# Attention for 64 heads on one core: pair 1 transposed head by head, score blocks dealt out anew, group 120 shared by two engines, a written order in place of a planner

## The chip, the cores and the metric

The kernel runs on one core of a Trainium2 chip. A core has five engines that run side by side, each with its own list of instructions: TensorE (PE in the profile, with its weight loads as PEld), VectorE (DVE), ScalarE (ACT), GpSimd (POOL) and SyncE (SP, which here only issues DMAs). The metric is the device time of one execution in microseconds; lower is better.

## The reference

For 64 heads (8 batches of 8) of 512 rows and 64 columns, in float32:

```python
scale = 1.0 / np.sqrt(q.shape[-1])
scores = np.einsum('bhqd,bhkd->bhqk', q, k) * scale
scores = scores - scores.max(axis=-1, keepdims=True)
attn = np.exp(scores)
attn = attn / attn.sum(axis=-1, keepdims=True)
return np.einsum('bhqk,bhkd->bhqd', attn, v).astype(np.float32)
```

## The kernel before

**Tiling.** Heads go in 32 pairs, a (h = 0) and b (h = 1). A pair's q and k are loaded as 256 KB each, cast to f16 by GpSimd (`cast`, L525), transposed by TensorE through an identity (`transposes`, L558) into PSUM, and copied by VectorE to `tqk` (`copy`, L571): 64 partitions for head a, 64 for head b. A score block is 128 keys by 512 queries of one head, one matmul with 64 contracted rows (`scores`, L598). Two blocks make a group of 128 x 1024 scores in one of three PSUM buffers `st`. In most pairs a group holds chunk c of head a and of head b, whose two matmuls lie in different row halves of the array; in pairs 0 and 31 it holds two chunks of one head. The 128 groups, 0 to 127, are taken in order; the last is done in two halves of 256 queries (numbers 127 and 128).

**Two ways to the exponential.** For 112 groups ScalarE reads `st` and writes `pt`, f16 (L602; L801 for the first three). For the 16 groups in `ON_DVE` VectorE does it from the bits of the number: `raise_` (L625) reads `st` and writes `pd`, then come five passes in SBUF (`pass_`, L642 to L665), which leave two factors, `pe` and `pd`, that TensorE uses as two blocks.

**Values.** A unit is 128 queries of one head: four matmuls of 65 columns (L704), one for each key chunk, and one more for each chunk that VectorE did. The 65th column sums the weights. Seven units fill a PSUM bank; VectorE takes a reciprocal (L671) and multiplies into a ring in SBUF (L676), from which SyncE stores. Values wait in the list until TensorE has time: `pt` has 24 buffers. The last head (31b) has its own matmuls (`last_values`, L720), reciprocal, product and store (L733, L734, L740); the two stores before it go out by ScalarE's queue.

**Order.** `Plan.run` steps through a model of the engines with fixed costs and writes the list of steps down; `do[what](*args)` (L867) issues them under a manual schedule, so that each engine works through its own part of that list in order. `KNOWN` names exponentials that also wait for an old GpSimd cast; a cast may be told to wait for a VectorE instruction (`cast_behind`, L539).

**Start.** Pair 0 is loaded by halves, and `first_pair` does its q and k through short steps of its own. Pair 1's q and k are loaded whole; k is cast by GpSimd, q half by VectorE (L523) and half by GpSimd (L524); k and q of both heads are transposed and copied one after the other (L565), and the first scores of pair 1 (group 4) need all of it.

Of the kernel before, what the change touches and what calls it, by code (L numbers as in the profile page):

```python
# [17 lines left out]
class Plan:  # L18

    SLOT, EXP, EXP_DONE, EXP_FIXED = 216, 853, 181, 64  # L20
    INTO, OUT_OF = 96, 96
    TRANSPOSE, V_UNIT = 222, 128
    TO_ACT, TO_DVE, TO_PE = 220, 210, 60

    COPY, NORM, RAISE = (601, 690), (50, 133), (1132, 1215)
    RECIPROCAL = 115
    SCALE, PRODUCT, EXTRA = 333, 600, 29
    COPY_1 = (400, 190)
    NORM_COLUMN, PASS_DONE = 67, 115
    PASSES = (SCALE, SCALE, PRODUCT, SCALE, PRODUCT)  # L30
    BITS = 2
    NEEDS = (None, None, 0, 2, 3)
    FIRST_EXP = 5000
    STEP = 5
    CALM, KEEN = 9000, 4
    FIRST_UNIT = 4
    KNOWN, OVER = (13, 15, 18, 20, 22, 24, 27, 42, 50, 61, 69, 97), 6
    ON_DVE = (5, 10, 16, 25, 28, 39, 44, 54, 63, 66, 74, 81, 91, 96, 103, 116)

    LATE_NORM, LATE_COPY, HURRY, SOON, BACKLOG = 700, 1500, 800, 160, 600  # L40
    LATE_MUL, WAIT = 400, 200
    SLACK, AHEAD = 0, 2

    CAST, CAST_PORT, CAST_DONE, TO_POOL = 557, 475, 130, 150
    SCALE_PORT, PRODUCT_PORT, GAP, REACH = 271, 537, 20, 5
    FIRST_LAND, LOAD, STORE, LATENCY, ISSUE = 5200, 752, 376, 2300, 470
    QUEUED, URGENT = 3500, 16
    PAIRED, STORE_ISSUE = 18, 520
    RAW, QK16, NV, NU = 7, 5, 12, 112
    PAIR, DUEK, DUEV, DUEL, PRE = 3300, 3550, 6000, 5000, 0  # L50

    def __init__(self, groups, pairs, first):
        self.groups, self.pairs = groups, pairs
        self.pe, self.act, self.dve = 7000, self.FIRST_EXP, 6300
        self.pool, self.port, self.dma = 4600, 4600, self.FIRST_LAND
        self.m, self.tiled = first, True
        self.read = []
        self.exps = {}
        for m in range(first):
            self.act += self.EXP + self.EXP_FIXED  # L60
            self.exps[m] = self.act + self.EXP_DONE
            self.read.append(self.exps[m])
        self.tq = {0: 5800}
        self.transposed = {0: 5800}
        self.next_t = 1
        self.part_t = 0
        self.banks = [5100, 5800]
        self.todo = [(g, h) for g in range(pairs) for h in range(2)]
        self.last = self.todo.pop()
        self.last_part = 0  # L70
        self.head = None
        self.units = self.FIRST_UNIT
        self.member = {b: m for m, grp in enumerate(groups) for b in grp}
        self.ready = []
        self.passes = []
        self.passed = {}
        self.raised = set()
        self.steps = []
        self.busy_dve = 0
        self.order, self.paired = [], 0  # L80

        late = {grp[0][0] for m, grp in enumerate(groups) if m in self.ON_DVE}
        due = []
        for g in range(pairs):
            scores = 5000 + self.PAIR * g
            if g:
                due += [(scores - self.DUEK, g, "k"), (scores - self.DUEK + 10, g, "q")]
            due.append((scores + self.DUEV + (self.DUEL if g in late else 0), g, "v"))
        self.due = sorted(due)
        self.uncast = list(self.due)  # L90
        self.casts = []
        self.landed, self.cast_done = {}, {}
        self.first_loads = [(g, n) for _, g, n in self.due if g < self.RAW]
        self.first_loads += [(self.RAW, "k"), (self.RAW, "q")]
        for x in self.first_loads:
            self.dma += self.LOAD
            self.landed[x] = self.dma
        self.loads, self.stores, self.stored = [], [], []
        self.sp = 1650 + 470 * len(self.first_loads)

    def note(self, t, *what):
        self.steps.append((t, len(self.steps)) + what)

    def trigger(self, t):

        ops = self.ops
        if not ops or ops[-1][1] <= t - 300:  # L110
            return 1, None
        n = len(ops) - 1
        while (
            n > 0
            and len(ops) - n < self.REACH
            and not ops[n][2]
            and ops[n][0] - ops[n - 1][1] <= self.GAP
        ):
            n -= 1
        if n > 0 and ops[n][0] - ops[n - 1][1] <= self.GAP:  # L120
            n -= 1
        return len(ops) - n, ops[n][1]

    def emit(self, t, back, after):
        _, g, n = self.uncast.pop(0)
        shared = (g, n) == (1, "q")
        self.note(t, "cast", g, n, back if t > self.CALM else 0)
        if not shared:
            self.casts.append((g, n, t if after is None else after + self.TO_POOL))
        if g + self.RAW < self.pairs:  # L130
            self.loads.append((g + self.RAW, n))

    def fits(self, t, soon=0):
        if not self.uncast:
            return False
        _, g, n = self.uncast[0]
        if n != "v" and g >= self.QK16 and self.transposed.get(g - self.QK16, 1e9) > t:
            return False
        return self.landed.get((g, n), 1e9) <= t + soon

    def step_pool(self, t):
        if self.uncast and self.uncast[0][1:] != (1, "q") and not self.casts and self.pool <= t:
            quiet = not self.passes and self.port <= t and not any(x[1] == "raise" for x in self.ready)
            if self.fits(t) and (quiet or self.uncast[0][0] - self.PRE < t):
                self.emit(t, 1, None)
        if self.casts and self.pool <= t and self.port <= t:
            g, n, after = self.casts[0]
            if after <= t and self.landed.get((g, n), 1e9) <= t:
                self.casts.pop(0)
                begin = max(self.pool, self.port, after, self.landed[(g, n)])  # L150
                self.pool = begin + self.CAST
                self.port = begin + self.CAST_PORT
                self.cast_done[(g, n)] = begin + self.CAST + self.CAST_DONE

    def step_sp(self, t):
        if self.sp > t or (self.loads and self.dma > t + self.QUEUED):
            return
        urgent = len(self.stores) > self.URGENT
        if self.loads and not urgent:
            g, n = self.loads[0]  # L160
# [7 lines left out]
        if self.stores and self.stores[0] <= t:  # L168
            both = self.both()
            if both and (len(self.stores) < 2 or self.stores[1] > t):  # L170
                return
# [26 lines left out]
    def free(self, n=0):  # L198
        m = self.m + n
        if m >= len(self.groups):  # L200
            return 1e9
# [697 lines left out]
```

## Time and profile before

| what | value |
|---|---|
| median of 3 runs | 113.71 us (113.62 to 113.92) |
| profiled execution | 113.92 us |
| its span, first to last instruction | 112.1 us |
| PE busy, share of span | 103.2 us, 92% |
| DVE busy | 100.8 us, 90% |
| ACT busy | 105.5 us, 94% |
| POOL busy | 65.9 us, 59% |
| granted TensorE clock | 0.994 |

The profiled execution takes 1.8 us more than its span; a change of the span is taken as the same change of the time. A row of the timeline has the start of a run of equal instructions, how long it takes from the first start to the last end, and behind x their count; records of one engine may overlap, since the next instruction enters while the last one drains. In a row of the stretches (windows) the busy time of an engine stands beside the count of its instructions.

### The profile page before, as it was taken

The page shows a single profiled execution, that of the slowest core. Times are in us where ns is not written, and L with a number is a line of the kernel's source. Part 1 is how long each engine was busy: PE and PEld are TensorE (multiplying, and loading weights), DVE is VectorE, ACT ScalarE, POOL GpSimd, SP SyncE. Part 2 cuts the span into 40 slices and gives each one's busy share as a digit, 9 for nine tenths or more (in the row PEclk, how much of TensorE's full clock was granted, in tenths as well). Part 3 has the DMA queues.
Part 4 walks back from the last instruction along what each step waited for, and adds up shares of the span by engine and source line. Part 5 has one row for each costly group of instructions (what it writes and reads, how often), then busy time and mean ns, then how long its engine had stood idle before and what let it go on. Part 6 is the DMA issues. An engine that isn't in the chain of part 4 may idle for free.

```text
span 112.1 us, 4408 instructions
## 1 busy us (share of the span) xinstructions
PE 103.2 (92%) x1728; PEld 69.4 (62%) x1728; DVE 100.8 (90%) x227; ACT 105.5 (94%) x118; POOL 65.9 (59%) x127
## 2 busy tenths in 40 slices
PE   7978889999799998999989999899999999999980
PEld 7634555766367766658647767577557577675660
DVE  1647999999999999999999999999999999997390
ACT  4599999999999999999999999999999999999970
POOL 2147768549756886495594786876784855600000
PEclk9999999999999999999999999999999999999997
DMA  3999999999999999999999999999999974142354
GB/s 106 276 359 353 345 350 347 355 336 349 345 347 336 341 346 343 354 364 375 370 358 382 350 355 377 354 372 362 343 366 305 349 245 143 52 141 99 97 167 161
DMA packets 35093, 33.84 MB, mean 302 GB/s; under 512 B 2304, under 2 KB 35072, under 8 KB 35072
## 3 DMA queue, kind: packets, MB, share of 16 engines
q1 hardware_dynamic: 34496, 33.04, 90.4%
q10 hardware_dynamic: 576, 0.52, 1.4%
q8 instruction: 13, 0.21, 0.8%
q14 instruction: 8, 0.07, 0.2%
HBM read 25.17 MB, written 8.39 MB: 299 GB/s over the span
## 4 chain that ended last, share of the span: by engine, by line
DVE 39%; PE 24%; DMA 15%; issue 8%; POOL 7%; SPq 3%; ACT 2%; POOLq 0%; ACTq 0%
PE o L704 13%; DMA v<-in_v_dram 10%; PE st L598 8%; DVE pd L625 8%; DVE tqk L571 7%; DVE ring L676 7%; DMA q<-in_q_dram 5%; DVE m L659 4%; POOL qkp L525 4%; DVE pd L665 4%; POOL vp L515 3%; PE tp L558 2%; SPq L509 2%; DVE m L642 2%; DVE pe L651 2%
## 5 line engine op out<-in xcount | busy, mean ns | idle before, releaser
L602 ACT ACTIVATE pt<-st 128x1024 f16<-128x1024 f32 (+1 forms) x110 | 100.3, 1144 | 0.2 <-PE st L598 0.2
L704 PEld LDWEIGHTS <-pt 128*128 128x128 f16 x880 | 38.8, 98 | 12.1 <-issue 10.2
L704 PE MATMUL o<-vp,pt 128*128 128x65 f16 x880 | 45.3, 194 | 0.4 <-POOL vp L515 0.2
L598 PE MATMUL st<-tqk 64*128 64x512 f16 (+1 forms) x250 | 41.7, 380 | 2.6 <-ACT pt L602 1.4
L525 POOL CAST qkp<-k 128x512 f16<-128x512 f32 x31 | 22.2, 717 | 11.3 <-DVE rc L671 5.3
L525 POOL CAST qkp<-q 128x512 f16<-128x512 f32 x30 | 21.7, 725 | 9.0 <-DVE rc L671 5.3
L515 POOL CAST vp<-v 128x512 f16<-128x512 f32 x32 | 21.4, 679 | 9.2 <-PE st L598 2.4
L676 DVE TENSOR_TENSOR ring<-o,rc 128x448 f32<-128x448 f32 (+2 forms) x37 | 22.3, 606 | 0.4
L704 PE MATMUL o<-vp,pe 128*128 128x65 f16 x128 | 21.8, 194 | 0.0
L704 PE MATMUL o<-vp,pd 128*128 128x65 f16 x128 | 21.7, 192 | 0.0
L558 PE MATMUL tp<-ident,qkp 128*128 128x128 f16 x248 | 19.6, 220 | 1.6 <-DVE tqk L571 0.8
L558 PEld LDWEIGHTS <-qkp 128*128 128x128 f16 x248 | 14.4, 97 | 9.9 <-issue 4.6
L571 DVE COPY tqk<-tp 128x1024 f16<-128x1024 f16 x30 | 20.3, 683 | 0.0
L625 DVE TENSOR_SCALAR pd<-st 128x1024 uint16<-128x1024 f32 x16 | 19.5, 1216 | 0.7 <-PE st L598 0.7
L598 PEld LDWEIGHTS <-tqk 64*128 64x128 f16 x250 | 10.7, 93 | 11.8 <-issue 4.6
L704 PEld LDWEIGHTS <-pe 128*128 128x128 f16 x128 | 12.5, 98 | 3.4 <-issue 3.3
L704 PEld LDWEIGHTS <-pd 128*128 128x128 f16 x128 | 12.5, 98 | 0.0
L659 DVE TENSOR_TENSOR m<-m 128x1024 f16<-128x1024 f16 x16 | 11.0, 685 | 0.0
L665 DVE TENSOR_TENSOR pd<-pd,m 128x1024 f16<-128x1024 f16 x16 | 10.9, 684 | 0.0
L671 DVE RECIPROCAL rc<-o 128x7 f32<-128x7 f32 (+2 forms) x37 | 7.4, 199 | 2.6 <-PE o L704 2.4
L661 DVE TENSOR_SCALAR m<-m 128x1024 f16<-128x1024 f16 x16 | 6.7, 418 | 0.1
L651 DVE TENSOR_SCALAR pe<-pd 128x1024 uint16<-128x1024 uint16 x16 | 6.6, 411 | 0.0
(51 smaller groups left out, 34.9 us busy)
## 6 DMA issues: line engine op xcount, KB each, us to landing
v<-in_v_dram SPq DMA_DIRECT2D x32, 256.0 KB, 5.8
k<-in_k_dram SPq DMA_DIRECT2D x31, 256.0 KB, 5.8
q<-in_q_dram SPq DMA_DIRECT2D x31, 256.0 KB, 5.9
out_dram<-ring SPq DMA_DIRECT2D x18, 256.0 KB, 5.5
out_dram<-ring SPq DMA_DIRECT2D x25, 128.0 KB, 2.2
k<-in_k_dram ACTq DMA_DIRECT2D x2, 128.0 KB, 2.8
q<-in_q_dram SPq DMA_DIRECT2D x2, 128.0 KB, 2.6
out_dram<-ring ACTq DMA_DIRECT2D x2, 128.0 KB, 1.9
```

The costliest lines, as they stand in the source:

```text
L515: return nc.gpsimd.tensor_copy(out=vps[g % NV][:, :, :, 0:D], in_=raw[g]["v"][:, :, :, :])
L525: return nc.gpsimd.tensor_copy(out=dst, in_=src[:, :, :, :])
L558: reads[g] = nc.tensor.transpose(tps[g][:, n, i, :], qkp[g][:, n, i, :], ident)
L571: nc.vector.tensor_copy(out=tqk[g][:, :, :], in_=tps.pop(g).rearrange("p n i c -> p n (i c)"))
L598: nc.tensor.matmul(st[:, x, cols], kc, qc[:, cols], start=True, stop=True)
L602: ins = nc.scalar.activation(out=pt[:, :, cols], in_=st[:, :, cols], func=EXP, scale=scale, bias=SHIFT)
L625: nc.vector.tensor_scalar(out=r["pd"][:, :, :], in0=r["st"][:, :, :], scalar1=BITS, scalar2=BIAS, op0=AluOp.mult, op1=AluOp.add,)
L651: ins = nc.vector.tensor_scalar(out=r["pe"][:, :, :], in0=u[:, :, :], scalar1=0x7C00, scalar2=None, op0=AluOp.bitwise_and,)
L659: ins = nc.vector.tensor_tensor(out=m16, in0=m16, in1=m16, op=AluOp.mult)
L665: ins = nc.vector.tensor_tensor(out=u16, in0=u16, in1=m16, op=AluOp.mult)
L676: nc.vector.tensor_tensor(out=ring[:, u % NU : u % NU + n, :], in0=o[:, x : x + n, 0:D], in1=rcs.pop(u)[:, 0:n].broadcast_to([P, n, D]), o ...
L704: nc.tensor.matmul(os[u // 7][:, u % 7, :], part[:, y * P : (y + 1) * P], vps[g % NV][:, h, c, :], start=(n == 0), stop=(n == len(parts) - 1),
```

## The change

The planner is taken out. A class `Order` holds the list of steps as text, one letter a step (S scores, T transposes, V a value unit, R raise, a to o the passes, C copy, N and M reciprocal and product, K cast, G load, w and W stores), with tables of what each takes. All orders differ from before. Counted in the two lists, TensorE enters a run of score matmuls 74 times before and 86 times now, and has 1152 and 1148 value matmuls in all.

- Pair 1: k and q are loaded by heads, k of a, q of a, k of b, q of b, on SyncE's queue. GpSimd casts k of each head, VectorE q of each head (step D). Head a's k and q are transposed into 64 partitions of a PSUM bank and copied together, then head b's.
- Groups of pair 1 are a0a1, a2b0, a3b1, b2b3, so that group 4 needs head a alone. Those of pair 31 are a0b0, a1b1, a2a3, b2b3; before they were a0a1, a2a3, b0b1, b2b3.
- `ON_DVE` has 16 other groups, the last three 103, 108 and 120. In 120 ScalarE does block a0 (`own` = 1, 128 x 512) and VectorE b0.
- `pe` and `pd` are taken from their pools at the raise, and a pass may stand later among the five (c is before b in most).

```diff
+    ON_DVE = (5, 11, 15, 26, 31, 38, 47, 55, 58, 70, 81, 84, 96, 103, 108, 120)
+    SPLIT = (120,)
+    PAIR_1 = "a0a1 a2b0 a3b1 b2b3"
+    LAST_PAIR = "a0b0 a1b1 a2a3 b2b3"
+    STEPS = (
+        "KDKTDSCTKSCKSSKRTTSKCVVVaSNcVSSKMVbTTdKSCKRSKVTSeTSCSKVVgTKRSGTKVGSKCVSGNfSkTTKGMShVGVmS"
...
+        "VowSVVRwVVVVNVaScSMVVVdwKSNVbVMVVVVeVwSNSMwVVVVwVVVwSNVMVVVLLwwNLLMFw"
...
+            if g == 1 and name in "kq":
+                halves.append((load_tile(g, name), source(src, g)))
+                if len(halves) == 2:
+                    for h in range(2):
+                        for t, rows in halves:
+                            nc.sync.dma_start(out=t[:, h], in_=rows[:, h])
+                continue
...
+        if g == 1:
+            h = "kq".index(name)
+            return nc.gpsimd.tensor_copy(out=rounded(1, "k")[:, h], in_=raw[1]["k"][:, h])
...
+    def cast_queries(h):
+        dve(nc.vector.tensor_copy(out=rounded(1, "q")[:, h], in_=raw[1]["q"][:, h]))
...
+    def head_transposes(h, bank):
...
+        cols = slice(0, 64 + 64 * h)
+        t = ps_x.tile([P, 2, NI, P], FP16, tag=f"x{bank ^ h}", name=f"tp_1_{h}")
+        for n in (1, 0):
+            for i in range(NI):
+                reads[1] = nc.tensor.transpose(t[cols, n, i, :], qkp[1][:, n, i, cols], ident)
+        flips.append(t)
...
+            h = len(copied)
+            rows = slice(64 * h, 64 * h + 64)
...
+                        out=tqk[1][rows, :, :], in_=flips[h][rows].rearrange("p n i c -> p n (i c)")
...
+        own = 0 if on_dve and m not in Order.SPLIT else 1 if on_dve else 2
...
-            blocks[(g, c, h)] = [part[:, x, :] for part in parts] if on_dve else [pt[:, x, :]]
-        if on_dve:
+            if x < own:
+                blocks[(g, c, h)] = [pt[:, x, :]]
+        if own == 0:
             return
...
-            out=pt[:, :, cols], in_=st[:, :, cols], func=EXP, scale=scale, bias=SHIFT
+            out=pt[:, 0:own, cols], in_=st[:, 0:own, cols], func=EXP, scale=scale, bias=SHIFT
...
-                out=r["pd"][:, :, :],
-                in0=r["st"][:, :, :],
+                out=r["pd"][:, own:2, :],
+                in0=r["st"][:, own:2, :],
```

Where the change moves instructions, first VectorE at pair 1's start. Before: half of q is cast (`qkp`), the transposed k and q are copied (`tqk`, 512 columns of 128 partitions each), then group 5 is raised and pair 2 copied.

```order
L523 CAST qkp_275<-q_1_110 128x2x2x64
L565 COPY tqk_284<-tp_0_285 128x512
L565 COPY tqk_284<-tp_1_293 128x512
L625 TENSOR_SCALAR pd_307<-st_305 128x1024
L571 COPY tqk_317<-tp_0_318 128x1024
```

Now:

```order
L241 CAST qkp_277<-q_1_109 128x4x64 x2
L281 COPY tqk_281<-tp_0_282 64x1024
L281 COPY tqk_281<-tp_1_298 64x1024
L350 TENSOR_SCALAR pd_326<-st_316 128x1024
L288 COPY tqk_328<-tp_329 128x1024
```

Both casts of q stand ahead of the first copy now, and a copy takes one head's k and q, 1024 columns of 64 partitions, in place of k or q of both heads.

Second, ScalarE near the end. Before, groups 117 to 121, after group 116 on VectorE:

```order
L602 ACTIVATE pt_2715<-st_2714 128x1024
L602 ACTIVATE pt_2738<-st_2737 128x1024
L602 ACTIVATE pt_2754<-st_2753 128x1024
L602 ACTIVATE pt_2761<-st_2760 128x1024
L602 ACTIVATE pt_2809<-st_2808 128x1024
```

Now, the same five groups:

```order
L321 ACTIVATE pt_2667<-st_2666 128x1024
L321 ACTIVATE pt_2714<-st_2713 128x1024
L321 ACTIVATE pt_2719<-st_2718 128x1024
L321 ACTIVATE pt_2770<-st_2769 128x512
L321 ACTIVATE pt_2777<-st_2776 128x1024
```

Every row was a full group; group 120 is a row of 512 columns now, because VectorE has its other block.

Third, VectorE near the end. Before, from the raise of its last group, 116, to that group's last pass, with the copy of pair 31 and two reciprocals and products between:

```order
L625 TENSOR_SCALAR pd_2701<-st_2699 128x1024
L571 COPY tqk_2721<-tp_0_2722 128x1024
L642 TENSOR_SCALAR m_2758<-pd_2701 128x1024
L651 TENSOR_SCALAR pe_2700<-pd_2701 128x1024
L659 TENSOR_TENSOR m_2758<-m_2758 128x1024
L671 RECIPROCAL rc_2793<-o_2685 128x7
L661 TENSOR_SCALAR m_2758<-m_2758 128x1024
L676 TENSOR_TENSOR ring<-o_2685,rc_2793 128x448
L671 RECIPROCAL rc_2819<-o_2771 128x7
L676 TENSOR_TENSOR ring<-o_2771,rc_2819 128x448
L665 TENSOR_TENSOR pd_2701<-pd_2701,m_2758 128x1024
```

Now, from the last pass of group 108 to the last of group 120:

```order
L393 TENSOR_TENSOR pd_2485<-pd_2485,m_2679 128x1024
L350 TENSOR_SCALAR pd_2813<-st_2769 128x512
L399 RECIPROCAL rc_2835<-o_2761 128x7
L370 TENSOR_SCALAR m_2842<-pd_2813 128x512
L387 TENSOR_TENSOR m_2842<-m_2842 128x512
L404 TENSOR_TENSOR ring<-o_2761,rc_2835 128x448
L389 TENSOR_SCALAR m_2842<-m_2842 128x512
L399 RECIPROCAL rc_2879<-o_2820 128x7
L379 TENSOR_SCALAR pe_2812<-pd_2813 128x512
L404 TENSOR_TENSOR ring<-o_2820,rc_2879 128x448
L393 TENSOR_TENSOR pd_2813<-pd_2813,m_2842 128x512
```

VectorE's last group of exponentials stands eight groups before the end of the order in place of twelve, at half the columns; three pairs of reciprocal and product follow its last pass in place of four, not counting the last head's own.

544 lines of the change are left out of this document (128 added, 416 removed), and 13 rows, old and new, of tables (CASTS, HEADS, LOADS).

## The prediction

> **What bounds the kernel now.** I read the stretches first, engine by engine for the middle of the run (start:end, length, then busy time and instruction count of each engine):
>
> ```profile
> 14.00:98.00 84.00, 81.02 (x1374) 54.33 (x1374) 83.68 (x174) 84.00 (x92) 58.92 (x112) 1.00 1.02 333
> ```
>
> PE 81.02, PEld, DVE 83.68, ACT 84.00 of 84.00 us: ScalarE is never idle here, VectorE for 0.32, TensorE for 2.98. The clock is 1.00 and plays no part. Three full engines do not tell which sets the end, so I read ScalarE's timeline whole, then in short windows that cut out single exponentials:
>
> ```profile
> 5.20 0.60 ACT L801 ACTIVATE pt<-st_0a 128x512 f16<-128x512 f32 x1 [0.43 <-PE st_0a L794]
> 5.69 0.59 ACT L801 ACTIVATE pt<-st_0b 128x512 f16<-128x512 f32 x1
> 6.17 1.95 ACT L801 ACTIVATE pt<-st 128x1024 f16<-128x1024 f32 x2
> 7.98 1.06 ACT L602 ACTIVATE pt<-st 128x1024 f16<-128x1024 f32 x1
> 9.21 99.28 ACT L602 ACTIVATE pt<-st 128x1024 f16<-128x1024 f32 x109 [0.18 <-PE st L598]
> 9.21 1.02 ACT L602 ACTIVATE pt<-st 128x1024 f16<-128x1024 f32 x1 [0.18 <-PE st L598]
> 10.13 1.02 ACT L602 ACTIVATE pt<-st 128x1024 f16<-128x1024 f32 x1
> 11.09 1.02 ACT L602 ACTIVATE pt<-st 128x1024 f16<-128x1024 f32 x1
> 12.01 96.48 ACT L602 ACTIVATE pt<-st 128x1024 f16<-128x1024 f32 x106
> 107.39 1.10 ACT L602 ACTIVATE pt<-st 128x512 f16<-128x512 f32 x2
> ```
>
> Records overlap, so ends are compared. The two halves of the first group end at 5.80 and 6.28, 0.48 apart; the two of the last take 1.10 where one takes 0.60: a half costs 0.49. From the end at 13.03 (12.01 + 1.02) to 108.49 lie 95.46 us with 103 full exponentials and two halves: (95.46 - 0.98) / 103 = 0.917 each. Where one ends later than that after its predecessor, ScalarE waited: 9.04 to 10.23 is 1.19, so 0.28 too much; 11.15 to 12.11 is 0.96, so 0.04. After that the 106 run at 0.917 to the end. ScalarE therefore has 0.32 us of waits in all, and its work alone gives 108.49.
>
> What follows is a chain with nothing to spare:
>
> ```profile
> 107.49 0.68 PE L704 MATMUL o<-vp,pt 128*128 128x65 f16 x16
> 108.01 0.84 PE L720 MATMUL o_last<-vp,pt 128*128 128x65 f16 x16
> 108.43 0.42 DVE L676 TENSOR_TENSOR ring<-o,rc 128x256 f32<-128x256 f32 x1
> 108.89 0.18 DVE L733 RECIPROCAL rc_last<-o_last 128x4 f32<-128x4 f32 x1
> 109.10 0.42 DVE L734 TENSOR_TENSOR obl<-o_last,rc_last 128x256 f32<-128x256 f32 x1
> 109.55 0.33 SPq L740 DMA_DIRECT2D out_dram<-obl  x1
> ```
>
> The last matmuls end 0.36 after the last exponential, the last reciprocal starts 0.04 later, the store 0.66 after that, and the span ends 2.55 after the store's issue: 3.61 in all. The code of these steps is unchanged. So the end moves with ScalarE's list, unless TensorE falls behind it.
>
> **The change part by part.**
>
> Group 120. ScalarE had 16 groups taken off it and now has 15 and a half: one instruction of 128 x 512 more, at 0.49: **+0.49**. Nothing hides it, since ScalarE waits for nobody after 12.1. VectorE is relieved of half a group:
>
> ```profile
> L625 DVE TENSOR_SCALAR pd<-st 128x1024 uint16<-128x1024 f32 x16 | 19.5, 1216 | 0.7 <-PE st L598 0.7
> L659 DVE TENSOR_TENSOR m<-m 128x1024 f16<-128x1024 f16 x16 | 11.0, 685 | 0.0
> ```
>
> About 0.6 of the raise, 0.3 of this pass and as much again of the other four; that shortens no wait on ScalarE's chain, as after 12.1 there is none, so I count it at nothing. If the later place of its last passes were not covered it would cost; the cover is VectorE's idle time near the end, 0.88 before its reciprocal at 104.03 and 1.48 before that at 106.37:
>
> ```profile
> 104.03 0.21 DVE L671 RECIPROCAL rc<-o 128x7 f32<-128x7 f32 x1 [0.88 <-PE o L704]
> 106.37 0.20 DVE L671 RECIPROCAL rc<-o 128x7 f32<-128x7 f32 x1 [1.48 <-PE o L704]
> ```
>
> The Trainium skill, ScalarE: Activation LUTs, section What ACT_TABLE_LOAD costs, gives 280 ns and 0.833 ns a column for an activation with a bias held per partition, less some 93 ns of overlap: by it the extra piece would be an estimated 0.61, and the sum 0.12 higher. The trace agrees with the slope ((0.917 - 0.49) / 512 = 0.834 ns) and not with the rest (0.06 us), and decides.
>
> The start of pair 1. The rows:
>
> ```profile
> 4.73 0.28 DVE L817 CAST q<-q 128x256 f16<-128x256 f32 x1
> 4.95 0.29 DVE L820 COPY qt<-tp_qb 128x256 f16<-128x256 f16 x1
> 6.65 0.62 POOL L525 CAST qkp<-k 128x512 f16<-128x512 f32 x1 [2.98 <-DMA k<-in_k_dram]
> 7.37 0.29 DVE L523 CAST qkp<-q 128x256 f16<-128x256 f32 x1 [1.15 <-DMA q<-in_q_dram]
> 7.76 0.97 DVE L565 COPY tqk<-tp 128x512 f16<-128x512 f16 x2
> 8.15 0.62 POOL L525 CAST qkp<-k 128x512 f16<-128x512 f32 x1 [0.23 <-DMA k<-in_k_dram]
> 8.78 0.82 PE L598 MATMUL st<-tqk 64*128 64x512 f16 x6 [0.52 <-DVE tqk L565]
> L571 DVE COPY tqk<-tp 128x1024 f16<-128x1024 f16 x30 | 20.3, 683 | 0.0
> ```
>
> Casts wait for loads at 6.65, 7.37 and 8.15, so 256 KB arrive every 0.75 and a half every 0.37: k of a about 6.28, q of a 6.65, k of b 7.0, q of b 7.37, all bytes of the pair when they came before. VectorE casts both q ahead of the first copy, so head a's copy follows the cast that starts at 7.37, 0.22 later (as 4.95 follows 4.73): 7.59. At 0.68 for 1024 columns it ends at 8.27, and group 4 starts at 8.32 (8.73 to 8.78 before). Its two blocks are of one head, in one half of the array, so one after the other: 0.39 and 0.22 more, 8.93, and the exponential at 8.97 in place of 9.21. It would end at 9.99; without a wait it would be 9.96. Of the 0.28 some 0.03 is left. The 0.04 further on came from group 7, whose scores stood behind values; they follow pair 2's transposes directly now. Together **-0.28**; the ends are -0.32 (all) and 0 (q of b lands later than its whole load did). SyncE issues two more DMAs, 0.47 each,
>
> ```profile
> 3.65 0.47 SPq L509 DMA_DIRECT2D v<-in_v_dram  x1
> 9.64 0.62 POOL L515 CAST vp<-v 128x512 f16<-128x512 f32 x1
> ```
>
> and the loads behind them go out 0.9 later; v, issued at 3.65, is used at 9.64, so the transfers in the queue ahead hide this. Uncovered it would be 0.9 on group 8.
>
> TensorE near the end. The prices:
>
> ```profile
> 97.24 0.43 PE L704 MATMUL o<-vp,pt 128*128 128x65 f16 x8
> 97.60 0.39 PE L598 MATMUL st<-tqk 64*128 64x512 f16 x2
> 97.93 0.62 PE L558 MATMUL tp<-ident,qkp 128*128 128x128 f16 x8
> 102.58 0.98 PE L598 MATMUL st<-tqk 64*128 64x512 f16 x4
> 104.87 0.61 PE L598 MATMUL st<-tqk 64*128 64x512 f16 x4
> 105.73 0.38 PE L598 MATMUL st<-tqk 64*128 64x256 f16 x2 [0.25 <-ACT pt L602]
> 106.04 1.20 PE L704 MATMUL o<-vp,pt 128*128 128x65 f16 x32
> 98.12 1.14 ACT L602 ACTIVATE pt<-st 128x1024 f16<-128x1024 f32 x1
> ```
>
> A value matmul is (1.20 - 0.19) / 31 = 0.0326, with 0.19 as what the last one takes; a transpose (0.62 - 0.22) / 7 = 0.057; a score group 0.61 - 0.39 = 0.22. Into a run of scores 97.60 - 97.24 - 8 x 0.0326 = 0.10 are lost, out of it 0.33 - 0.22 = 0.11: 0.2 for each run. From group 117's scores (97.60) to the end the list had 176 value matmuls, 8 transposes and 7 runs; now 222, 4 and 8, and one group fewer with its blocks after each other (group 124, 0.21). That is 1.50 - 0.23 + 0.2 - 0.21 = 1.26 more, while ScalarE has 0.43 less there (a half for a full). TensorE must be 1.69 further ahead. It gives up what it waited, 0.16 in the row at 102.58, 0.41 ahead of 105.73 and 0.16 within the 0.84 of the last 16: 0.73. And group 117 can come earlier: with 116 on VectorE it could lead by one exponential, 0.92 less the 0.05 from a release to the scores, and led by 0.52 (97.60 against 98.12); now 114 to 116 are all ScalarE's, and three buffers allow two, 1.78. If it again stays 0.35 below, that is 0.9 more. 1.63 against 1.69: short by 0.06. The values of head 31a now need group 126 in place of 125, which ends at 107.51 against their start at 107.49: with that on the product at 108.43 some 0.04. **+0.1**; the ends are 0 and 0.96 (no earlier group 117).
>
> TensorE ahead of that. 11 more runs at 0.2, two more same-head groups at 0.22 and 50 value matmuls fewer: 2.2 + 0.44 - 1.63 = 1.0, in the 2.98 that it has free between 14 and 98. Hidden if it falls between the scores' due times: 0; not hidden at all: 1.0. ScalarE waits nowhere there in the trace, so I take a value near the lower end, **+0.14**.
>
> The Trainium skill, TensorEngine Tiling (Array Packing), section Tiling Modes, says that a change of tiling mode drains TensorE, which speaks against more runs. It gives no figure; the 0.2 above are this trace's price for it.
>
> Sum: 0.49 - 0.28 + 0.1 + 0.14 = +0.45. The span of the profiled execution goes from 112.1 to 112.55, its time from 113.92 to 114.37; that execution was the slowest of the three, 0.21 above their median, so on the median 113.71 + 0.45 = **114.15**.
>
> **The rivals.** Faster or slower means by more than 0.3%, 0.34 us, about what a measurement of this kernel can tell from no change.
>
> (1) TensorE keeps up everywhere. Then only ScalarE's account is left, 0.49 - 0.28 + 0.04 = +0.25: 113.96, no change that counts. For it: 2.98 us of room in the middle, and the later values were only late because nothing hurried them. Against it: the 1.69 at the end has almost no room. From 0.09 of further waits on it is no longer this case.
>
> (2) TensorE becomes the bound, by its changes into and out of score runs. With half of the ends above (1.0 and 0.96) unhidden: 0.25 + 0.98, 114.94; with all, 115.9. For it: VectorE is full too, so a late copy or raise cannot be made up. Against: the extra work is a third of the room.
>
> (3) The halves of pair 1 do not come earlier, or the copy of head a waits longer. Then the wait at 9.21 stays: +0.73, 114.45.
>
> (4) Faster. ScalarE's list is 0.49 longer and has only 0.32 of waits to lose, so this needs 0.5 us off the start ahead of 5.20 or off the 3.61 behind the last exponential. No row offers it.
>
> **How the numbers follow.** Forecast 0.47, with its own range of 114.0 to 114.5, a quarter of it below 114.05; (1) 0.27; (2) 0.13; (3) 0.08; (4) 0.05. Same: 0.27 and 0.12, together 0.39. Slower: 0.35 + 0.13 + 0.08 = 0.56. Faster 0.05. The range goes from 113.85, below (1) by the spread of the runs, to 115.0, which leaves out the worse half of (2).
>
> **What would show it.** One more exponential, of 128 x 512, ending 0.49 after its predecessor. The first one of pair 1 near 8.97, with VectorE's second cast of q near 7.37. The last exponential's end near 108.7 if TensorE keeps up, 108.8 to 108.9 by the forecast. Spacings above 0.917 after 12 us would show TensorE or VectorE late; a last matmul more than 0.4 behind the last exponential would show the end short of TensorE. I am wrong if ScalarE's spacing is not constant, or if its last exponential ends before 108.6.

## The result, and the profile after

The changed kernel takes 115.46 us (median of 4 runs, 114.76 to 115.78) against 113.81 us for the kernel before on the same chip (4 runs, 113.62 to 114.36): a ratio of 1.0136, interval 1.0099 to 1.0172, so 1.1 to 2.0 us more. The forecast was 114.15. A profiled execution of it took 114.76, its fastest run, with a span of 113.0 in place of 112.1.

The stretch from 14 to 98 us, as before engine by engine (busy time and instruction count of PE, PEld, DVE, ACT, POOL; then clock, share of the DMA engines, GB/s):

```profile
14.00:98.00 84.00, 82.46 (x1344) 54.22 (x1345) 82.48 (x167) 83.74 (x93) 55.67 (x111) 1.00 1.01 333
```

TensorE does 1.44 us more here than before, VectorE 1.20 less, and ScalarE, which was never idle, is idle for 0.26. ScalarE's timeline shows where, and that it is the only place:

```profile
4.97 0.60 ACT L529 ACTIVATE pt<-st_0a 128x512 f16<-128x512 f32 x1 [0.29 <-PE st_0a L522]
7.75 6.56 ACT L321 ACTIVATE pt<-st 128x1024 f16<-128x1024 f32 x7
14.57 94.16 ACT L321 ACTIVATE pt<-st 128x1024 f16<-128x1024 f32 x104 [0.26 <-PE st L316]
```

Group 3 and the groups of pairs 1 and 2 run without a break from 7.75: the wait ahead of pair 1 is gone. A wait stands ahead of group 12 instead, at 14.57: ends are 1.284 apart there, 0.37 too much, where the wait at pair 1 had been 0.29 and the next one 0.05. After that 104 exponentials, three of them of 512 columns (the block of group 120 and the two halves of the last group), run to 108.73.

VectorE at pair 1's start, and the end (all engines):

```profile
6.80 0.29 DVE L241 CAST qkp<-q 128x256 f16<-128x256 f32 x1 [0.60 <-DMA q<-in_q_dram]
7.05 0.68 DVE L281 COPY tqk<-tp 64x1024 f16<-64x1024 f16 x1
```

```profile
108.43 0.66 PE L448 MATMUL o_last<-vp,pt 128*128 128x65 f16 x16
108.85 0.42 DVE L404 TENSOR_TENSOR ring<-o,rc 128x256 f32<-128x256 f32 x1
109.19 0.17 DVE L461 RECIPROCAL rc_last<-o_last 128x4 f32<-128x4 f32 x1
109.40 0.42 DVE L462 TENSOR_TENSOR obl<-o_last,rc_last 128x256 f32<-128x256 f32 x1
109.85 0.33 SPq L468 DMA_DIRECT2D out_dram<-obl  x1
```

Head a's copy starts at 7.05, half a microsecond earlier than forecast. At the end the last matmuls finish 0.36 behind the last exponential, as before. The last store is issued at 109.85, 0.30 later than before, and lands (the trace's event that its transfer is complete) after 1.72 (1.71 before). But the span then goes on to 112.98: 1.42 behind the landing, where it was 0.84.

The two spans, cut at the same four points, add up as follows (us; the landing and the ends are the trace's own events):

| stretch | before | after | difference |
|---|---|---|---|
| start to the first exponential | 5.20 | 4.97 | -0.22 |
| first exponential's start to the last one's end | 103.30 | 103.76 | +0.46 |
| last exponential's end to the last store's issue | 1.06 | 1.12 | +0.06 |
| issue to landing | 1.71 | 1.72 | +0.01 |
| landing to the end of the span | 0.84 | 1.42 | +0.58 |
| span | 112.10 | 112.98 | +0.89 |

The first row is spread: in five profiles with the new order and halves the first exponential starts at 4.97 to 5.44, 5.20 on average, 0.8 to 1.1 behind the landing of the last of pair 0's halves. The half exponential and the longer end come again in the second profile below; the waits between 8 and 20 us vary.

### The profile page after: what moved, and what is told of

Its sections match the earlier page's. It is cut to its first block, busy times and chain, and to the rows that moved or that the text cites. A ratio compares the mean times of both kernels' runs of the same rounds, so it can differ in the third digit from the quotient of the medians.

```text
span 113.0 us, 4387 instructions
## 1 busy us (share of the span) xinstructions
PE 105.7 (94%) x1732; PEld 70.3 (62%) x1732; DVE 102.5 (91%) x228; ACT 105.9 (94%) x119; POOL 62.2 (55%) x127
## 4 chain that ended last, share of the span: by engine, by line
PE 51%; DVE 30%; ACT 10%; issue 3%; DMA 2%; SPq 0%; ACTq 0%
PE o L432 22%; PE st L316 19%; ACT pt L321 10%; PE tp L263 8%; DVE pd L350 7%; DVE tqk L288 6%; DVE ring L404 5%; DVE m L387 3%; DMA q<-in_q_dram 2%; DVE pd L393 2%; DVE pe L379 2%; DVE m L370 2%; DVE rc L399 1%; DVE m L389 1%; PE tp L272 1%
## 5 line engine op out<-in xcount | busy, mean ns | idle before, releaser
L432 PE MATMUL o<-vp,pt 128*128 128x65 f16 x884 | 48.2, 195 | 0.2
L316 PE MATMUL st<-tqk 64*128 64x512 f16 (+1 forms) x250 | 44.0, 381 | 1.4 <-DVE tqk L288 0.8
L226 POOL CAST qkp<-q 128x512 f16<-128x512 f32 x30 | 20.0, 667 | 10.7 <-DVE rc L399 7.0
L226 POOL CAST qkp<-k 128x512 f16<-128x512 f32 x30 | 19.8, 661 | 6.9 <-DVE rc L399 2.3
L350 DVE TENSOR_SCALAR pd<-st 128x1024 uint16<-128x1024 f32 (+1 forms) x16 | 19.0, 1185 | 0.6 <-PE st L316 0.6
L316 PEld LDWEIGHTS <-tqk 64*128 64x128 f16 x250 | 11.6, 93 | 11.0 <-DVE tqk L288 2.0
L387 DVE TENSOR_TENSOR m<-m 128x1024 f16<-128x1024 f16 (+1 forms) x16 | 11.3, 714 | 0.0
L393 DVE TENSOR_TENSOR pd<-pd,m 128x1024 f16<-128x1024 f16 (+1 forms) x16 | 10.6, 663 | 0.0
L370 DVE TENSOR_SCALAR m<-pd 128x1024 uint16<-128x1024 uint16 (+1 forms) x16 | 6.9, 437 | 0.0
L379 DVE TENSOR_SCALAR pe<-pd 128x1024 uint16<-128x1024 uint16 (+1 forms) x16 | 6.6, 425 | 0.0
```

The costliest lines, as they stand in the source:

```text
L226: return nc.gpsimd.tensor_copy(out=dst, in_=src[:, :, :, :])
L316: nc.tensor.matmul(st[:, x, cols], kc, qc[:, cols], start=True, stop=True)
L350: nc.vector.tensor_scalar(out=r["pd"][:, own:2, :], in0=r["st"][:, own:2, :], scalar1=BITS, scalar2=BIAS, op0=AluOp.mult, op1=AluOp.add,)
L370: ins = nc.vector.tensor_scalar(out=r["m"][:, own:2, :], in0=u[:, own:2, :], scalar1=0x03FF, scalar2=0x3C00, op0=AluOp.bitwise_and, op1=Al ...
L387: ins = nc.vector.tensor_tensor(out=m16, in0=m16, in1=m16, op=AluOp.mult)
L393: ins = nc.vector.tensor_tensor(out=u16, in0=u16, in1=m16, op=AluOp.mult)
```

## The experiments

Each ratio is to the kernel before, run on the same chip in the same set of runs (its medians there were 113.71 to 114.06).

**The changed kernel once more.** No edit. A second profile and more runs.

> The changed kernel once more, for its spread and a second profile. In its first profile the last exponential ended at 108.73 us, 0.24 us later than before, the last store landed at 111.57 and the span ended 1.43 us after that (before: 0.84). Theory A (ScalarE waits in places that differ from run to run): a profile with a longer span has more or larger spacings above 0.917 us between the ends of exponentials, and the last exponential ends at 109.2 us or later. Theory B (the loss lies behind the last store): the last exponential ends at 108.6 to 108.9 us and 1.4 us or more lie between the last landing and the end of the span. Time 115.0 to 115.8 us by both.

115.27 (114.87 to 115.32, 6 runs), ratio 1.0097 [1.0070, 1.0124]. Its profiled execution starts the first exponential at 5.44; the waits between 7 and 16 us are five small ones, 0.45 in all, none of them at group 12 alone (0.06 there). From landing to end it is 1.42 again. The last exponential ends at 109.27, theory A's mark, but 0.46 of the 0.54 that it is later is the later start and 0.08 the waits. So the waits change their places from run to run, as theory A says, and the loss behind the landing stays, as theory B says.

**Group 120 not shared.**

```diff
-    SPLIT = (120,)
+    SPLIT = ()
```

> Group 120 goes to VectorE whole, as the other 15 groups; all else as in the changed kernel. If ScalarE's list sets the time: 0.49 us less than the changed kernel in the same call (a ratio of 0.996 to it). If VectorE or TensorE sets it near the end: no less, or more, with spacings above 0.917 us after group 120.

117.30 (116.69 to 117.57), ratio 1.0274 [1.0243, 1.0306]. ScalarE's timeline near the end, and TensorE's at the place where it stops:

```profile
108.46 2.07 ACT L321 ACTIVATE pt<-st 128x1024 f16<-128x1024 f32 x3 [1.89 <-PE st L316]
```

```profile
107.53 0.20 PE L432 MATMUL o<-vp,pd 128*128 128x65 f16 x1 [0.92 <-DVE pd L393]
```

This is the second expectation. Value matmuls that use VectorE's factor wait for VectorE's last pass, and the scores behind them in TensorE's list make ScalarE wait 1.89. In this order the sharing costs ScalarE 0.49, and without it the kernel is 2.0 slower (117.30 against 115.27).

**Group 116 shared in the kernel before.** The same sharing, in the old order.

```diff
+        own = 0 if on_dve and m != 116 else 1 if on_dve else 2
...
-            out=pt[:, :, cols], in_=st[:, :, cols], func=EXP, scale=scale, bias=SHIFT
+            out=pt[:, 0:own, cols], in_=st[:, 0:own, cols], func=EXP, scale=scale, bias=SHIFT
```

> The kernel before, with its own order; only VectorE's last group, 116, is shared: ScalarE takes its first block. If ScalarE's list sets the time: one exponential of 0.49 us more, 114.3 us. If the relief of VectorE pays it back: 113.8 us or less.

114.40 (113.97 to 115.94), ratio 1.0038 [1.0011, 1.0066]: +0.43, 0.1 to 0.75, as expected if ScalarE's list sets the time. The half exponential ends 0.490 after its predecessor. Landing to end is 0.84, so the end does not come from the sharing.

**Pair 1 head by head in the kernel before.** Its order, `ON_DVE` and last pair; of the change only the loads by halves, the casts, transposes and copies of pair 1 and its groups. TensorE also takes group 7's scores ahead of the eight value matmuls that stood before them, as the change does.

```diff
+    PAIR_1 = 'a0a1 a2b0 a3b1 b2b3'
...
+                    for h in range(2):
+                        for t, rows in halves:
+                            nc.sync.dma_start(out=t[:, h], in_=rows[:, h])
...
+        dve(nc.vector.tensor_copy(out=rounded(1, "q")[:, h], in_=raw[1]["q"][:, h]))
```

> The order, the groups on VectorE and pair 31 of the kernel before; only pair 1 is loaded, cast, transposed and copied head by head, with its groups a0a1, a2b0, a3b1, b2b3. If the head-by-head start does what was forecast: no spacing of 1.19 us at the first exponential of pair 1, ScalarE's last exponential 0.28 to 0.32 us earlier than before relative to its first. Two more loads move the last store from the last to the second of the semaphores that SyncE waits for at the end, and four more waits of 0.06 us follow its landing: 0.25 us. In sum 113.7 to 113.8 us, no change. If the late copies of pair 1 cost more behind it: a spacing above 1.2 us between 10 and 16 us, and 114.1 us or more.

114.56 (114.23 to 115.41), ratio 1.0061 [1.0035, 1.0088]. GpSimd, then TensorE:

```profile
8.01 0.61 POOL L327 CAST qkp<-k 128x512 f16<-128x512 f32 x1 [1.31 <-DMA k<-in_k_dram]
9.78 0.61 POOL L327 CAST qkp<-q 128x512 f16<-128x512 f32 x1 [1.16 <-DMA q<-in_q_dram]
```

```profile
10.45 0.40 PE L364 MATMUL tp<-ident,qkp 128*128 128x128 f16 x4 [0.84 <-POOL qkp L327]
10.78 0.60 PE L417 MATMUL st<-tqk 64*128 64x512 f16 x2
```

Pair 1 starts without a wait, but pair 2's q lands at 9.73 (8.85 before), GpSimd waits 1.16 for it, TensorE 0.84 for the cast, and group 7's scores stand behind those transposes: ScalarE loses 0.94 there. The end behind the landing is 1.06 here, between 0.84 and 1.42: it has two causes, and one of them comes with pair 1.

**Pair 3's copy earlier in the changed kernel.** VectorE's first product goes ahead of pass c, and pair 3's copy ahead of pass d.

```diff
-        "KDKTDSCTKSCKSSKRTTSKCVVVaSNcVSSKMVbTTdKSCKRSK...
+        "KDKTDSCTKSCKSSKRTTSKCVVVaSNMcVSSKVbTTCKdSKRSK...
```

> The changed kernel with VectorE's work around 12 us in another order: product of the first bundle of values ahead of the square (pass c), and the copy of pair 3 ahead of pass d in place of behind it. Nothing else differs. Theory: the lead won at pair 1 was given back because group 12's scores waited 0.46 for pair 3's copy (start 13.39), which stood behind a product and three passes; its transposes (12.75) had waited for that product too. Then the copy starts near 13.0 or earlier, group 12's exponential ends 0.92 after its predecessor in place of 1.28, and the time falls by 0.3 to 0.4, from 115.3 to 114.95. Rival: the loads set the pace here, since the core's transfers give no more; then a wait of about the same size shows up at pair 3 or 4 again, group 12 to 16, and the time stays within 0.1 of 115.3.

115.47 (114.83 to 115.66), ratio 1.0113 [1.0057, 1.0168]: nothing gained. In the profile of the changed kernel the wait at group 12 had come about like this (VectorE, then TensorE):

```profile
12.26 0.34 DVE L404 TENSOR_TENSOR ring<-o,rc 128x192 f32<-128x192 f32 x1
13.39 0.69 DVE L288 COPY tqk<-tp 128x1024 f16<-128x1024 f16 x1
```

```profile
12.75 0.61 PE L263 MATMUL tp<-ident,qkp 128*128 128x128 f16 x8 [0.38 <-DVE ring L404]
14.14 0.39 PE L316 MATMUL st<-tqk 64*128 64x512 f16 x2 [0.46 <-DVE tqk L288]
```

The product frees the bank for pair 3's transposes, whose copy frees group 12's scores. But the list alone did not make this wait. Pass c, just ahead of the product, took 0.98 in that profile, where it had begun while GpSimd cast pair 3's q (VectorE, GpSimd); in the second profile of the same kernel it began behind the cast and took 0.69 (last row):

```profile
11.36 0.98 DVE L387 TENSOR_TENSOR m<-m 128x1024 f16<-128x1024 f16 x1
11.16 0.62 POOL L226 CAST qkp<-q 128x512 f16<-128x512 f32 x1
```

```profile
12.18 0.69 DVE L387 TENSOR_TENSOR m<-m 128x1024 f16<-128x1024 f16 x1
```

In the three profiles of this order in which pass c took 0.98 (the first, group 120 not shared, the eight memsets below) group 12 waited 0.31 to 0.37; in the three in which it took 0.69 (the second, and the two with pair 1 loaded whole below), 0.06. So most of this wait goes with the meeting of the two engines, and it is not there in every execution of the same list. With both steps moved up, group 12 no longer waits, and group 16, the first of pair 4, does (VectorE, TensorE, ScalarE):

```profile
14.24 0.83 DVE L389 TENSOR_SCALAR m<-m 128x1024 f16<-128x1024 f16 x1
16.72 0.68 DVE L288 COPY tqk<-tp 128x1024 f16<-128x1024 f16 x1
```

```profile
17.45 0.38 PE L263 MATMUL tp<-ident,qkp 128*128 128x128 f16 x4 [0.23 <-DVE tqk L288]
```

```profile
18.20 1.94 ACT L321 ACTIVATE pt<-st 128x1024 f16<-128x1024 f32 x2 [0.41 <-PE st L316]
```

0.51 is lost there, behind pair 4's copy. VectorE has no idle time from 14.2 to 18.9 in this profile, and pass d at 14.24, again with a cast of GpSimd under way, took 0.83, where it took 0.41 in the first profile of the changed kernel. That the wait comes back is as the rival said; that the loads are why is not shown here, since the row names VectorE.

**Eight more memsets on GpSimd, in the changed kernel.**

```diff
         if part == 0:
+            for _ in range(8):
+                nc.gpsimd.memset(mark[0:1, :], 0.0)
```

> The changed kernel with eight more one-row memsets on GpSimd, put behind its last cast, where it is idle. No other engine's list differs. In three profiles of this program GpSimd's second event behind the last drain came 0.37 after the first (111.98 to 112.35), against 0.06 to 0.07 in the three with the old order; GpSimd has 202 records in the one and 215 in the other, so its 197th falls at the very end in the one and at 86 to 92 us, off the path, in the other. Theory: the gap belongs to a place in GpSimd's list of instructions (a piece of code that is not there yet); with eight more ahead of it, it falls on the memsets, the two events come 0.06 apart and the time falls by 0.31, to 114.95, though work was added. Rival: the gap belongs to this moment (what the other engines have just done); then it stays at 0.37 and the time at 115.3.

114.99 (114.35 to 115.74), ratio 1.0090 [1.0054, 1.0127], though waits of 0.84 stand between 10 and 16 us in its profile (pair 2's q lands at 9.62). Work was added and the end got shorter: landing to end 1.06. Events of GpSimd in the exchange of signals with which all engines end (the last barrier), start and end in us from the span's start:

```
changed kernel      111.964-111.981   112.353-112.370
eight memsets more  112.703-112.720   112.786-112.803
```

The 0.37 between them is 0.07 now. The view of the DMA queues shows what else differs. From 111 us on, the changed kernel has a packet in an instruction queue:

```profile
q14 instruction: 1, 0.01, 0.8%
```

and with the eight memsets there is none behind 111 us, as in the kernel before. But this packet is not what the pause waited for: it starts at 113.06, 0.7 behind the end of the pause and behind the end of the span. GpSimd's list has 202 records in the new order in place of 215, and the pause stands ahead of the 197th; with the memsets the 197th is one of them, and no pause of this size stands there. That the pause hangs on the length of the list is shown by the run; what the engine waits for in it stays open.

**Pair 1 loaded whole in the changed kernel.** Two loads in place of four; 144 DMAs in place of 146.

```diff
-                if len(halves) == 2:
-                    for h in range(2):
-                        for t, rows in halves:
-                            nc.sync.dma_start(out=t[:, h], in_=rows[:, h])
+                t, rows = halves[-1]
+                nc.sync.dma_start(out=t[:, :, :, :], in_=rows)
```

> The changed kernel with pair 1's k and q loaded whole again (two loads of 256 KB in place of four halves); casts, transposes and order as changed. 144 DMAs in place of 146. Theory: SyncE ends with eight waits in a fixed order, one for each of eight counters that the DMAs take in turn; with 146 the last store is on the counter waited for second, and four waits of 0.06 each follow its landing; with 144 it is on the last one. So the stretch from the last store's landing to the end of the span falls by 0.25, from 1.43 to 1.18. At the start pair 1's first exponential waits again (0.2 to 0.3, both halves of q land at 7.1 to 7.4), and the wait at group 12 shrinks by as much. Time 114.9 to 115.1. Rival: the number of DMAs doesn't matter for the end; then 1.43 stays and the time is 115.2 to 115.5.

114.88 (114.10 to 116.15), ratio 1.0091 [1.0065, 1.0118]. Landing to end is 1.19, 0.23 less: one of SyncE's waits ends behind the landing and not five (the four more start at 111.624, 111.688, 111.750 and 111.809 in the changed kernel, 0.06 apart). And the loads behind pair 1 come earlier: pair 2's q at 8.17, no wait over 0.13 between 8 and 16 us, 0.40 in all. The times alone tell neither this run nor the one with the memsets from the changed kernel (1.0091 and 1.0090 against 1.0097, with overlapping intervals); what each edit takes off the end is read from the traces.

**Pair 1 loaded by halves in the kernel before.** The same code as the change has it, nothing else.

> The kernel before with one edit: pair 1's k and q are loaded by heads (four halves); its casts, transposes, copies and the order stay, so the casts wait for both heads. 146 DMAs. Theory: loading by halves brings the bytes of pair 1 sooner (q of b at 6.4 to 6.9 in the profiles with halves, q whole at 7.1 to 7.4 in those without) but not those behind: pair 2's q landed at 8.6 to 9.7 with halves, 8.6 to 8.8 without, as the rate from 6 to 10 us was 285 to 335 GB/s against 350 to 370. Then the 0.28 of wait ahead of pair 1's first exponential goes, a wait of 0.2 to 0.9 comes at group 8 or 12, and with the four waits behind the last store (0.25) the time is 0.2 to 0.7 above before: 114.1 to 114.6. Rival: the waits further on come from the new order of VectorE's list alone; then nothing replaces the 0.28, and the time is 113.91 - 0.3 + 0.25, within 0.1 of before.

114.45 (113.86 to 115.43), ratio 1.0053 [1.0014, 1.0092]. The wait ahead of pair 1 is gone, and group 7's scores wait 0.45 too long, behind values that need pair 0's v (TensorE). Six waits of 0.03 to 0.21, 0.51 together, follow up to 42 us.

```profile
10.40 0.42 PE L712 MATMUL o<-vp,pt 128*128 128x65 f16 x8 [0.40 <-POOL vp L522]
10.76 0.39 PE L606 MATMUL st<-tqk 64*128 64x512 f16 x2
```

Landing to end is 1.06. The transfers from 5 to 10 us (last number GB/s), first of the changed kernel, then of this one, and of the kernel with pair 3 by halves, below:

```profile
5.00:10.00 5.00, 4.89 (x48) 2.65 (x44) 3.40 (x8) 5.00 (x7) 2.64 (x5) 1.00 0.98 313
```

```profile
5.00:10.00 5.00, 4.03 (x40) 1.99 (x37) 2.96 (x8) 4.83 (x7) 2.51 (x5) 1.00 0.99 317
```

```profile
5.00:10.00 5.00, 4.20 (x40) 2.24 (x38) 2.74 (x9) 4.70 (x7) 2.98 (x5) 1.00 1.06 344
```

In all eight profiles with pair 1 by halves the rate here is 301 to 320, in the six others 344 to 349.

**Pair 3 loaded by halves in the kernel before.** The edit is that of the run above, with `g == 3`.

> The kernel before with one edit: pair 3's k and q (the seventh and the eighth load that SyncE issues for pairs 1 to 3) are loaded by heads, four halves, where pair 1's were in an earlier run. 146 DMAs. Theory: smaller loads bring the rate down while they and those behind them are under way; then the transfers run at 350 to 370 GB/s up to 9.5 us and at 285 to 335 for two or three us behind, and loads from pair 4 on land 0.2 to 0.6 late. Rival: halves do no harm in a queue that is already full, and the holes of pair 1's halves come from the start, where little is under way; then the rate stays at 345 to 370, all loads land every 0.75, and the time is before plus the four waits behind the last store, 0.25.

114.01 (113.81 to 114.54), ratio 1.0031 [1.0015, 1.0046]: +0.35, 0.17 to 0.52, with landing to end 1.06. The rival holds: halves land every 0.37, wholes every 0.75, and nothing waits. Smaller loads alone do not slow the queue; at its start they do. Why there is open.

**Both pieces of the end taken off the changed kernel.** Pair 1 whole, and the eight memsets.

> The changed kernel with pair 1's k and q loaded whole (144 DMAs) and eight more memsets on GpSimd behind its last cast: both edits that each took a piece off the end. Theory: the two pieces are independent, so the stretch from the last store's landing to the end of the span is that of the kernel before, 0.84 to 0.86 (1.43 in the changed kernel, 1.19 with whole loads alone, 1.06 with the memsets alone), and what is left of the loss is the half exponential, 0.49, and the spread of the start: 0.4 to 0.7 above before. Rival: the new order costs time of its own in the middle (TensorE's extra runs of scores, the later passes); then spacings above 0.917 show up between 20 and 107 us, and it is 0.9 or more above before.

114.66 (113.97 to 115.72, 6 runs), ratio 1.0067 [1.0041, 1.0094]: 0.5 to 1.1 above before. Landing to end is 0.84, as before the change. Its profiled execution, the slowest of the six, started late (first exponential at 5.89), with waits of 1.07 in all up to 16 us and none from 17 us to the end, so the rival's waits in the middle are not there. The estimate falls between the two expectations, and its interval takes in both.

**Two queues at the start, kernel before.** ScalarE's queue issues pair 1's k.

```diff
-            nc.sync.dma_start(out=t[:, :, :, :], in_=source(src, g))
+            queue = nc.scalar if (g, name) == (1, "k") else nc.sync
+            queue.dma_start(out=t[:, :, :, :], in_=source(src, g))
```

> The kernel before with one edit: pair 1's k is issued by ScalarE's queue, behind its two loads of pair 0, in place of SyncE's; it is still one load of 256 KB, 144 DMAs in all. SyncE issues everything else 0.47 earlier. The cores' transfers fall from about 300 to 180 to 280 GB/s between 4 and 6 us in every profile. Theory: that dip comes from the issues, one each 0.47 to 0.51 on SyncE; with two queues issuing, pair 1's q lands 0.2 to 0.4 earlier than 7.35 less the start's spread, the wait ahead of pair 1's first exponential shrinks from 0.28 to 0.1 or less with no later wait taking its place, as the loads behind come earlier by as much: 0.2 below before. ScalarE's table load starts 0.45 later (1.67 to 2.1) and may hold up its first cast (3.09 to 3.40) by 0.1. Rival: the dip comes from the transfers themselves; then nothing lands earlier and the time is that of before, or up to 0.2 above where the table load delays the first exponential.

114.75 (114.33 to 115.91), ratio 1.0108 [1.0065, 1.0150]: slower. k lands at 7.41 (6.60 before) and q at 6.74 (7.35): they changed places, and the pair is complete no earlier. The wait ahead of pair 1 grows to 0.56. From 4 to 5 us the rate is 181 GB/s (276 before), though SyncE's other loads went out earlier: the dip is not made by the issues.

**The start by halves, mended.** The kernel before with halves, group 7's scores ahead of the two value units, and two pairs' stores merged so that there are 144 DMAs.

```diff
+        for one in (700, 684):
...
+            steps[one + 5] = ("store", 2)
+            del steps[one]
+        at = steps.index(("scores", 7, False))
+        steps.insert(at - 2, steps.pop(at))
```

> The kernel before with three edits: pair 1's k and q loaded by heads (as in an earlier run, which lost the 0.29 won at pair 1 again at group 7, whose scores stood behind values that waited for pair 0's v); group 7's scores moved ahead of those two value units on TensorE; and the stores of pairs 20 and 23 made whole pairs, so that there are 144 DMAs again and the last store is on the counter that is waited for last. Theory: the wait of 0.29 at pair 1 goes, the 0.45 at group 7 shrinks to 0.1 or less, and landing to end is 0.84 again: 0.1 to 0.3 below before, 113.45 to 113.65. Rival: VectorE, busy all the time from 9 us on, cannot follow; then what is won comes back as waits of 0.05 to 0.5 between 11 and 45 us (in the run with halves alone they were 0.5 in all behind group 7), and the time is that of before or up to 0.4 above. If q or v of pairs 2 and 0 land late again (after 8.9 and 9.7), it is above before too.

114.40 (113.86 to 114.64), ratio 1.0029 [0.9999, 1.0060]. Group 7 no longer waits and landing to end is 0.84, but q of b landed at 7.05, so pair 1 waited 0.44, and four waits of 0.02 to 0.14 came between 24 and 43 us. No version tried beats the kernel before.

## Why the prediction was wrong

**The end is the step that failed.** The prediction took "3.61 in all" from the last exponential to the end of the span, with the reason "The code of these steps is unchanged." The code is; the time is 4.26. Landing to end, over fourteen profiles, goes by two counts and nothing else:

| | 144 DMAs | 146 DMAs |
|---|---|---|
| GpSimd's list as before (215 or 217 records), or with eight memsets more (210) | 0.84 (five profiles) | 1.06 (four) |
| GpSimd's list as changed (202) | 1.19 (one) | 1.42 (four) |

Two more loads, made 110 us earlier, put the last store on another of eight counters that the DMAs take in turn; SyncE waits for the counters in a fixed order, so four waits stand behind the landing in place of none: +0.23. GpSimd's shorter list puts a pause of 0.37 in place of 0.07 into the last barrier, and a later step of that barrier takes 0.05 longer: +0.35. Together 0.58, of which the prediction had nothing; without it the median of 115.46 would be an estimated 114.88, within the range. Its fourth rival named "the 3.61 behind the last exponential" as a place that could move, but only as a gain.

**The start was right at its place and wrong in sum.** In the first profile the chain worked as described and even earlier: copy at 7.05 against 7.59, no wait at group 4. In the second the copy started at 7.94 and group 4 waited 0.14. The -0.28 was not kept. ScalarE's waits in all, one number for each profile:

| | pair 1 loaded whole | pair 1 by halves |
|---|---|---|
| old order | 0.33 (the kernel before), 0.22, 0.05 | 0.95, 1.15 (pair 1 head by head) |
| new order | 0.40, 1.07 (the late start) | 0.37, 0.45, 0.84, 1.00 (pair 3's copy moved) |

The kernel before with two queues had 0.61, the mended start 0.74, and the run without sharing is left out because its end waits.

The step that failed is "Of the 0.28 some 0.03 is left": the wait ahead of pair 1 was taken as won for the end. It was partly that one execution's. In the two other profiles of the old order that load pair 1 as before (group 116 shared, pair 3 by halves) the first exponential started 0.11 to 0.18 later, pair 1's q landed 0.26 to 0.38 earlier, and pair 1 did not wait. And what was won came back behind it, in ways that differ from profile to profile. In two profiles (pair 1 head by head, eight memsets) "the transfers in the queue ahead hide this" failed: pair 2's q landed at 9.73 and 9.62, and group 7 lost 0.94 and 0.51; the prediction's own price for the case was "0.9 on group 8". In three, pass c met GpSimd's cast, and group 12 lost 0.31 to 0.37. In the second profile, and with pair 1 loaded whole, small waits of 0.04 to 0.14 at several groups make up 0.45 and 0.40. The loads by halves were slower at the start (301 to 320 GB/s from 5 to 10 us against 344 to 349; pair 2's q at 8.5 to 9.7 against 8.2 to 8.9), and in the old order they cost waits; that they are the cause in the new order is not shown, since 0.40 is there with whole loads too. A term of -0.28 was really 0 to +0.7.

**The half exponential was right.** +0.49 in the sum; 0.490 between the ends in both kernels that share a group, +0.43 [0.1, 0.75] measured for it alone. The prediction's estimate of 0.61 by the Trainium skill (ScalarE: Activation LUTs, What ACT_TABLE_LOAD costs) took the section's price for a bias held per partition, but the kernel gives the bias as a number (`bias=SHIFT`). For that the same section of the Trainium skill has 186 ns in place of 280, an estimated 0.52 for the piece; 0.490 was measured, and the measurement decides.

**TensorE cost less than forecast.** Of the +0.1 near the end only 0.06 appeared, behind the last exponential (the product of head 31a at 108.85 keeps VectorE: the last reciprocal starts 0.10 behind the last matmul in place of 0.04); the last matmuls end 0.36 behind the last exponential, within the 0.4 given as the mark. Of the +0.14 ahead of that nothing appeared: TensorE did 1.44 more between 14 and 98 and no exponential waited for it after 15.6. Here rival (1) was right. That the values are ready depends on the sharing: without it VectorE's last pass was late by 0.92 and ScalarE lost 1.89.

**The sum.** 0.49 for the half exponential and 0.58 and 0.06 for the end make 1.13. The start (where the first exponential begins, and the waits) adds -0.18 in the first profile and +0.36 in the second. That gives 0.95 and 1.49, against spans that are 0.89 and 1.42 longer than before; the medians of the two sets of runs are 1.65 and 1.36 higher, and what the executions without a profile lost at the start is not known. The range failed at its top, 115.0, since the one mechanism that was missing was larger than the whole forecast of 0.45.

## What to carry to other kernels

The time behind the last store is part of the kernel: count the DMAs and the instructions of each list before and after, and see in the trace whether the last store's counter is waited for last and whether an engine pauses in the last barrier. A wait removed at the start is only worth what the next load and the next engine can follow; price it against the landing of the loads behind it, not against the wait alone, and see in a second profile whether the wait is there each time. Where two engines are as full as ScalarE and VectorE here, a wait that is mended can come back, as it did here one copy later.

## What the hardware showed unexpectedly

- A pause of 0.37 in GpSimd's last barrier (0.07 otherwise) hung on how many instructions its list had; eight one-row memsets in its idle time took it away. A packet of an instruction queue came and went with it, but started only behind the pause; what the pause waits for is open.
- Each further wait of SyncE, on counters that were already complete, took 0.06 behind the landing; four cost 0.23.
- Loading two 256 KB tensors as four halves lowered the rate from 344 to 349 GB/s to 301 to 320 over five microseconds when they were the first loads behind pair 0's, and not at all (344) a few loads later.
- The same pass of VectorE (128x1024, f16, two inputs) took 0.98 in place of 0.69 when it began while a cast of GpSimd was under way, in three profiles of six, and most of the wait at group 12 went with that.
